# Attention inside a four-layer hybrid model on one core: a unit's transpositions stand one cycle later, and its probabilities lie in free rows of another pool

## The chip, the cores and the metric

The kernel runs on one core of a Trainium2 chip, in one launch. The metric is the device time in microseconds of one execution, and the number compared is the median over several runs.

The engines have these names in the profile: PE is TensorE's matmul, PEld its weight loads, DVE is VectorE, ACT is ScalarE, POOL is GpSimd, and SP issues most of the DMAs. Each engine works through its own instructions in the order in which they stand, and waits for the others by semaphores.

## What is computed

A token sequence of 16 meta tokens and 1024 tokens passes through four layers with residual additions: sliding-window attention, mLSTM, HGRN2, and sliding-window attention again. All arithmetic is float32; the kernel forms a float32 product as three products of split operands (high by high, high by low, low by high). Only the two attention layers matter here. Cut to the mixing itself:

```python
A_HEADS, A_KV, A_HD, BLOCK = 16, 4, 64, 128

def sliding_window_attention(q, k, v, sinks, valid):
    # qb: [bsz, nb, BLOCK, A_KV, g, A_HD]; kk, vv: the block before and the block itself
    s = jnp.einsum('bnqhgd,bnkhd->bnhgqk', qb, kk) * (A_HD ** -0.5)
    s = jnp.where(mask[None, :, None, None], s, -jnp.inf)       # causal band of 128 tokens
    sink = sinks.astype(jnp.float32).reshape(A_KV, g, 1)
    m = jnp.maximum(s.max(axis=-1), sink)
    e = jnp.exp(s - m[..., None])
    p = e / (e.sum(axis=-1) + jnp.exp(sink - m))[..., None]
    o = jnp.einsum('bnhgqk,bnkhd->bnqhgd', p, vv)
    return o.reshape(bsz, lp, A_W)
```

Around it stand an RMS norm, the projections to q, k, v and a gate z, norms and rotary positions on q and k, `o * silu(z)`, and the projection back to 1024 columns.

## The kernel before

**How the work is tiled.** Tokens stand in three chunks of 400, 384 and 256 columns, and in nine blocks for the attention: block 0 has the 16 meta tokens, blocks 1 to 8 have 128 tokens each. Heads are taken four at a time. A *unit* is one block of queries and one *pair*: two q tiles `t` of 128 features with two heads each (`hh` 0 and 1, indexed by feature half; `u` 0 and 1, indexed by tile). Four pairs by nine blocks are 36 units in the first attention layer; the last layer leaves block 0 out and has 32.

**What a unit does.** Three steps, which the code calls by letters:

- `S_step` (the scores): PE makes the scores of the four heads in two PSUM banks `pm` (L959). POOL copies the heads' sinks beside the place of the scores (L969). DVE adds the mask and scales into the SBUF tile `Sm`, with the row minimum of the negated scores (L972, one instruction and a small read-out for each head). ACT takes the exponential with the row sum (L977, once for each head). DVE inverts the four sums (L979), and POOL multiplies the rows by them (L982, once for each `hh`, two heads at a time). What is then in `Sm` are the probabilities.
- `T_step` (the transpositions): for each `hh`, PE transposes the probabilities through the identity (L998), up to four matmuls of 128 columns, into a PSUM bank `pt`; ACT rounds them to the high part `Ph` (L1000) and DVE subtracts for the low part `Pl` (L1001).
- `V_step` (the values): PE multiplies v by `Ph` and `Pl` into `po` (L1016). After the last block of a group, ACT and DVE move the sums into the output rows `R["o", t]` (L1024, L1025).

**What sets the order.** PE's order is written out by the program: `mixers()` makes a list of steps with costs, in which empty steps with a cost are pauses, and `weave` merges that list with the *fill*, the projections of the same layer (L271 for q, k, v and z, L569 for the projection back), in proportion to the costs. So the pauses only say how much fill stands between two steps. One cycle of the list before, for the unit `d` whose scores are made and the unit `e` ahead of it:

```python
seg += both(432, T_step, e)
if d:
    seg.append([1000, hi(lambda d=d: S_step(d)), None])
seg.append([V_WAIT, lambda: None, None])     # 1000
seg += both(480, V_step, e)
if d:
    seg.append([T_WAIT, lambda: None, None])  # 1500
```

The other engines' orders are made from the same program by a scheduler with priorities. It also hands out buffers. `Sm` comes from the layer's own pool with 2 buffers, one for each `hh`, so that the next unit's sinks and scores wait until the transpositions of the unit ahead have read them. `row()` is another pool: eight rows of 1040 float32 columns, tag "r", that hold k's high and low parts, the output rows of the pairs under way, working rows of k's projection in the first layer, and some weights.

Of the kernel before, what the change touches and what calls it, by code (L numbers as in the profile page):

```python
# [9 lines left out]
F32 = mybir.dt.float32  # L10
F32R = mybir.dt.float32r
AF = mybir.ActivationFunctionType
ALU = mybir.AluOpType
PSUM = bass.MemoryType.PSUM

P = 128
D = 1024
KT = D // P
NMETA = 16
# [10 lines left out]
def blk(b):  # L30
    return (0, NMETA) if b == 0 else (NMETA + P * (b - 1), P)
# [13 lines left out]
KT_LAG, ATT_LAG = 1400.0, 600.0  # L45
NORM_AT = (4000.0, 0.7), (5000.0, 0.5), (8000.0, 0.5)
Y_LAST, Y_EARLY, Y_AHEAD = 3, 8, 2500.0
V_WAIT, T_WAIT = 1000.0, 1500.0
D_V, V_AHEAD, K_AHEAD = 1500.0, 6500.0, 12000.0
FIRST = (1.1, 0.2, 0.85), (2.1, 1.35, 1.85)  # L50
D_K0, D_K1 = (4300.0, 6300.0, 8300.0), (4400.0, 5700.0, 6700.0)
# [70 lines left out]
def hybrid_kernel(ctx: ExitStack, tc: tile.TileContext, ins, out, layers=(0, 1, 2, 3)):  # L122
    nc = tc.nc
    v, s, g, pe, sp = nc.vector, nc.scalar, nc.gpsimd, nc.tensor, nc.sync
# [11 lines left out]
    def nm(x):  # L136
        ctr[0] += 1
        return f"{x}{ctr[0]}"

    def row():  # L140
        return rpool.tile([P, T], F32, tag="r", name=nm("r"), bufs=ROWS)
# [10 lines left out]
    def small(w):  # L152
        return tpool.tile([P, w], F32, tag=f"s{w}", name=nm("s"), bufs=12 if w < 8 else 4)

    def psum(tag, bufs):
        return ps.tile([P, 512], F32, tag="p", name=nm(tag), bufs=8)
# [59 lines left out]
    def new_mix():  # L216
        if layer_pool[0] is not None:
            layer_pool[0].close()
        layer_pool[0] = ExitStack()
        return layer_pool[0].enter_context(tc.tile_pool(name=nm("mix"), bufs=1))  # L220
# [59 lines left out]
    def hi(fn):  # L280
        def f():
            with tc.high_priority(offset=PRIO):
                fn()

        return f
# [442 lines left out]
    def layer_a(i, j, first, last, fin, scale=None):  # L728
        win, wout = ins["a_win"][j], ins["a_wout"][j]
        chunks = LAST_CHUNKS if last else CHUNKS  # L730
        R = {}

        def enter():
            R["mix"] = mix = new_mix()
            R["masks"] = masks = mix.tile([P, 384], F32, name=nm("masks"))
            sp.dma_start(masks, ins["a_masks"])
            R["cons"] = cons = mix.tile([P, 18], F32, name=nm("cons"))
            sp.dma_start(cons, ins["a_cols"][j])
            v.tensor_scalar(cons[:, 0:1], cons[:, 0:1], -0.125, None, op0=ALU.mult)
            v.tensor_scalar(cons[:, 2:18], cons[:, 2:18], -1.0, None, op0=ALU.mult)  # L740
# [45 lines left out]
        def idle(n, c0, cn):  # L786
            z = [R["mix"].tile([P, 2, 2, P], F32, tag=z, name=nm(z), bufs=2) for z in ("Ph", "Pl")]
            z = [y.rearrange("p a u q -> p (a u q)") for y in z]
            z.append(R["mix"].tile([P, 2, 257], F32, tag="Sm", name=nm("Sm"), bufs=2).rearrange("p u k -> p (u k)"))
            return [y[:, :cn] for y in z]  # L790

        def qk_proj(src, gcol, work, fsplit, ch, t=None, fetched=False):
# [142 lines left out]
        def mixers():  # L935


            def S_step(d):
                mix, cons = R["mix"], R["cons"]
                b, n, pair, ts = d[0]["b"], d[0]["n"], d[0]["pair"], d[0]["ts"]  # L940
                q0, nq = blk(b)
                kq = CHUNK_BLOCKS[n].index(b)
                qb = slice(q0 - chunks[n][0], q0 - chunks[n][0] + nq)
                if b == 0:
                    k0, kbs = 0, ((0, 0, 16),)
                elif b == 1:
                    k0, kbs = 0, ((0, 0, 16), (1, 16, 128))
                else:
                    k0, kbs = q0 - P, ((b - 1, 0, 128), (b, 128, 128))
                nk = sum(z[2] for z in kbs)  # L950
                kw, mo = (nk if b == 0 else 256), {0: 128, 1: 112}.get(b, 0)
                S = [psum("pm", 2).rearrange("p (u k) -> p u k", u=2) for _ in range(2)]
                k = R["k", pair // 2]
                for u, t in enumerate(ts):
                    q = R["q", t, n]
                    for i, (x, y) in enumerate(((0, 0), (0, 1), (1, 0))):
                        for hh in range(2):
                            hs = slice(64 * hh, 64 * hh + 64)
                            pe.matmul(S[hh][:nq, u, :kw], q[x][hs, qb], k[y][hs, k0 : k0 + kw],  # L959
                                      start=(i == 0), stop=(i == 2))  # L960
                st, den = small(8), small(8)
                for w in d:
                    hh = w["hh"]
                    w["kbs"] = kbs
                    w["Sm"] = Sm = mix.tile([P, 2, 257], F32, tag="Sm", name=nm("Sm"), bufs=2)
                    if b == 0:
                        g.memset(Sm[:, :, :NMETA], 0.0)
                    head = (2 * (ts[0] // 4) + hh) * 4 + ts[0] % 4
                    g.tensor_copy(Sm[:nq, :, nk : nk + 1], cons[:nq, 2 + head : 4 + head].rearrange("p (u c) -> p u c", c=1))  # L969
                    for u in range(2):  # L970
                        rq = R["rq", ts[u], n][:nq, 2 * kq + hh : 2 * kq + hh + 1]
                        v.tensor_tensor_reduce(Sm[:nq, u, :nk], S[hh][:nq, u, :nk], R["masks"][:nq, P + mo : P + mo + nk],  # L972
                                               rq, cons[:nq, 2 + head + u : 3 + head + u], ALU.add, ALU.min,
                                               st[:nq, 2 * hh + u : 2 * hh + u + 1])
                    for u in range(2):
                        z = slice(2 * hh + u, 2 * hh + u + 1)
                        s.activation(Sm[:nq, u, : nk + 1], Sm[:nq, u, : nk + 1], AF.Exp, scale=-1.0,  # L977
                                     bias=st[:nq, z], accum_out=den[:nq, z])
                v.reciprocal(den[:nq, :4], den[:nq, :4])  # L979
                for w in d:  # L980
                    hh, Sm = w["hh"], w["Sm"]
                    g.tensor_tensor(Sm[:nq, :, :nk], Sm[:nq, :, :nk],  # L982
                                    den[:nq, 2 * hh : 2 * hh + 2].rearrange("p (u c) -> p u c", c=1).to_broadcast([nq, 2, nk]),
                                    op=ALU.mult)

            def T_step(w):
                b, kbs, Sm = w["b"], w["kbs"], w["Sm"]
# [39 lines left out]
            units = []  # L1027
# [6 lines left out]
            def both(cost, fn, d):  # L1034
                return [[cost, hi(lambda w=w: fn(w)) if w else lambda: None, None] for w in d or (None, None)]

            for k in range(len(units) + 1):
                d = units[k] if k < len(units) else None
                e = units[k - 1] if k else None
                seg = segs[d[0]["pair"] if d else 4]  # L1040
                seg += both(432, T_step, e)
                if d:
                    seg.append([1000, hi(lambda d=d: S_step(d)), None])
                    if d[0]["b"] == CHUNK_BLOCKS[d[0]["n"]][-1]:
                        order["S", d[0]["pair"], d[0]["n"]] = seg[-1]
                seg.append([V_WAIT, lambda: None, None])
                seg += both(480, V_step, e)
                if d:
                    seg.append([T_WAIT, lambda: None, None])
            return segs  # L1050

        zc = {t: gate_proj(win[12 + t], lambda t=t: R["o", t], chunks, scale) for t in range(8)}
# [18 lines left out]
        head, ev = [], []  # L1071
        for n in range(3):
# [9 lines left out]
            head.append(grp)  # L1082
        hang = ev
        head[0].insert(0, [0.0, enter, None])
        sp1, out1 = outs(oc[1])
        sp3, out3 = outs(oc[3])
# [7 lines left out]
        ]  # L1094
        body = []
        segs = mixers()
        for p, ahead in enumerate((V_AHEAD, 0.0, K_AHEAD, 0.0)):
            segs[p].insert(0, [ahead, lambda: None, None])
# [5 lines left out]
        for i in range(3, 12):  # L1104
            for t in (2 * (i // 3), 2 * (i // 3) + 1):
                at = [id(z) for z in body]
                q, k = (at.index(id(z)) if id(z) in at else -1
                        for z in (order["q", t, i % 3], order["S", i // 3 - 1, i % 3]))
                if q < k:
                    z, d = body.pop(q), 0.0  # L1110
# [737 lines left out]
    for pos, i in enumerate(layers):  # L1848
# [10 lines left out]
        if i % 3 == 0:  # L1859
            head, body, oa, ob = layer_a(i, i // 3, tail is None, i == 3, fin, norm if tail is None else None)  # L1860
        elif i % 3 == 1:
            head, body, oa, ob = layer_b(i, i // 3, fin)
        else:
            head, body, oa, ob = layer_c(i, i // 3, fin)
        if tail is not None:
# [6 lines left out]
            h0, h1 = (sum(z[0] for z in head[k]) for k in range(2))  # L1872
            seq += flat(head)
            for n, start, end in ((2, t_b, t_b + h0 + h1), (1, t_a, t_b + h0), (0, 0.0, t_b)):
                d, share = NORM_AT[n]
                t0 = skip + start + d
                norm.place(seq, n, t0, t0 + 600.0, t0 + 600.0 + share * (skip + end - t0 - 600.0))
            head = [seq]
        else:
# [10 lines left out]
            head = [seq]  # L1890
# [16 lines left out]
    ahead, k = 0.0, 0  # L1907
# [120 lines left out]
```

## Time and profile before

| | |
|---|---|
| median of 3 runs | 2573.05 us (2572.45 to 2578.16) |
| the profiled execution: its own time | 2573.78 us |
| the profiled execution: its span | 2572.0 us |
| mean granted TensorE clock | 0.996 |
| first attention layer, units under way | from 59 us to about 425 us |
| last attention layer, units under way | from about 2168 us to 2505 us |

The span is what the profile covers, from the first instruction to the last; the execution's own time is 1.8 us longer. In the profile's rows, "x" gives a count. In a table of waits the columns are the total in us, how often, and the longest. In the table by stretches of time there are, after the bounds and the length, the busy us of each engine with the count of its instructions, then PEclk, the TensorE clock that was granted (1.00 is full), the share of the DMA engines and GB/s. A busy PE is not PE at its peak, and "idle before" is counted from the modelled end of the matmul ahead.

### The profile page before, as it was taken

What the parts mean: (1) busy time and instruction counts of PE and PEld (TensorE: products, weight loads), DVE (VectorE), ACT (ScalarE), POOL (GpSimd) and SP (SyncE); (2) the same over time, 40 slices, a digit from 0 to 9 for tenths busy, and PEclk for the clock granted to TensorE, in tenths of its full rate; (3) what the DMA queues carried; (4) which work ended last, traced back from release to release, by engine and by line L of the source; (5) the groups of instructions that cost most, each with busy time, mean ns of one, the idle gap of its engine ahead of it and who ended that gap; (6) DMA issues with size and microseconds to landing.
All of it is one profiled execution on the core that took longest, in us unless ns stands there. A gap on an engine that the chain in (4) does not pass through costs nothing.

```text
span 2572.0 us, 55550 instructions
## 1 busy us (share of the span) xinstructions
PE 2517.3 (98%) x20424; PEld 2438.9 (95%) x20424; DVE 2122.4 (83%) x5804; ACT 1733.9 (67%) x4679; POOL 252.1 (10%) x569
## 2 busy tenths in 40 slices
PE   9899999999999999999999999999999999999999
PEld 8799998999999999999999999999999999899989
DVE  7786887988979889789887798888878988787876
ACT  7665767576877778778772248887676856756672
POOL 0321222000000000000000001100000100321220
PEclk9999999999999999999999999999999999999999
DMA  5113222212212222221242211110111113112212
GB/s 164 51 55 89 60 64 65 87 53 50 71 45 73 68 55 62 59 73 52 84 126 91 66 50 35 35 40 30 43 35 43 39 47 100 50 49 76 60 34 82
DMA packets 113714, 161.58 MB, mean 63 GB/s; under 512 B 16521, under 2 KB 65810, under 8 KB 113442
## 3 DMA queue, kind: packets, MB, share of 16 engines
q1 hardware_dynamic: 113154, 157.51, 20.5%
q8 instruction: 161, 2.64, 0.4%
q14 instruction: 111, 0.91, 0.1%
q10 hardware_dynamic: 288, 0.52, 0.1%
HBM read 132.48 MB, written 14.92 MB: 57 GB/s over the span
## 4 chain that ended last, share of the span: by engine, by line
PE 58%; DVE 20%; ACT 13%; DMA 4%; issue 3%; POOL 1%; SPq 0%; DVEq 0%; POOLq 0%; ACTq 0%
PE pj L271 17%; PE pj L569 15%; PE pj L387 9%; PE pj L530 4%; PE pj L472 2%; DMA wr<-in_b_win 2%; ACT Sm L977 2%; PE pt L998 2%; DVE wl L231 2%; ACT wh L230 1%; POOL Sm L982 1%; ACT t L706 1%; ACT t L705 1%; PE po L1016 1%; PE pm L959 1%
## 5 line engine op out<-in xcount | busy, mean ns | idle before, releaser
L271 PE MATMUL pj<-uh,wh 128*128 128x384 f32 (+2 forms) x1680 | 572.9, 341 | 1.8 <-ACT uh L646 1.0
L271 PE MATMUL pj<-ul,wh 128*128 128x384 f32 (+2 forms) x1680 | 540.3, 322 | 1.5 <-DVE ul L647 1.0
L271 PE MATMUL pj<-uh,wl 128*128 128x384 f32 (+2 forms) x1680 | 539.9, 321 | 0.0
L271 PEld LDWEIGHTS pj<-uh,wh 128*128 128x128 f32 x1680 | 317.6, 189 | 15.1 <-issue 2.2
L271 PEld LDWEIGHTS pj<-ul,wh 128*128 128x128 f32 x1680 | 318.2, 189 | 5.6 <-DVE ul L647 1.6
L271 PEld LDWEIGHTS pj<-uh,wl 128*128 128x128 f32 x1680 | 317.4, 189 | 0.3 <-DVE wl L231 0.3
L231 DVE TENSOR_TENSOR wl<-wr,wh 128x512 fp32r<-128x512 f32 (+1 forms) x336 | 239.1, 721 | 72.5 <-ACT wh L230 69.0
L230 ACT CAST wh<-wr 128x512 fp32r<-128x512 f32 (+1 forms) x336 | 202.6, 614 | 90.4 <-DMA wr<-in_b_win 24.3
L572 DVE TENSOR_TENSOR x<-x,pj 128x384 f32<-128x384 f32 (+2 forms) x480 | 234.2, 510 | 35.0 <-PE pj L569 33.6
L569 PE MATMUL pj<-yh,wh 128*128 128x384 f32 (+2 forms) x768 | 253.8, 330 | 4.3 <-DVE x L572 4.0
L569 PE MATMUL pj<-yl,wh 128*128 128x384 f32 (+2 forms) x768 | 246.0, 320 | 0.3 <-DVE yl L231 0.3
L387 PE MATMUL pj<-uh,wh 128*128 128x384 f32 (+1 forms) x756 | 244.5, 323 | 1.3 <-ACT t L585 1.0
L569 PE MATMUL pj<-yh,wl 128*128 128x384 f32 (+2 forms) x768 | 245.3, 319 | 0.0
L387 PE MATMUL pj<-uh,wl 128*128 128x384 f32 (+1 forms) x756 | 238.7, 316 | 0.2 <-DVE wl L231 0.2
L387 PE MATMUL pj<-ul,wh 128*128 128x384 f32 (+1 forms) x756 | 238.4, 315 | 0.0
L982 POOL TENSOR_TENSOR Sm<-Sm,s 128x512 f32<-128x512 f32 (+2 forms) x136 | 143.4, 1075 | 433.3 <-DVE s L979 417.5
L977 ACT ACTIVATE Sm<-Sm,s 128x257 f32<-128x257 f32 (+2 forms) x272 | 129.8, 479 | 73.9 <-DVE s L972 72.7
L230 ACT CAST yh<-r 128x384 fp32r<-128x384 f32 (+2 forms) x120 | 57.0, 479 | 163.5 <-PE pj L569 146.5
L569 PEld LDWEIGHTS pj<-yh,wh 128*128 128x128 f32 x768 | 144.4, 188 | 7.9 <-DVE x L572 4.6
L708 ACT ACTIVATE t<-t 128x384 f32<-128x384 f32 (+3 forms) x240 | 117.7, 491 | 50.6 <-DVE t L707 48.8
L530 PE MATMUL pj<-wh,uh 128*128 128x256 f32 (+1 forms) x504 | 145.9, 290 | 0.0
L569 PEld LDWEIGHTS pj<-yl,wh 128*128 128x128 f32 x768 | 144.6, 188 | 1.0 <-DVE yl L231 0.7
(378 smaller groups left out, 6971.8 us busy)
## 6 DMA issues: line engine op xcount, KB each, us to landing
wr<-in_b_win SPq DMA_DIRECT2D x124, 256.0 KB, 2.8
wr<-in_a_win SPq DMA_DIRECT2D x78, 256.0 KB, 2.9
wr<-in_c_win SPq DMA_DIRECT2D x64, 256.0 KB, 2.6
wr<-in_a_wout SPq DMA_DIRECT2D x32, 256.0 KB, 3.0
rw<-rowsd SPq DMA_DIRECT2D x64, 128.0 KB, 3.7
wr<-in_b_wout SPq DMA_DIRECT2D x32, 256.0 KB, 2.8
parked<-r SPq DMA_DIRECT2D x12, 520.0 KB, 2.6
r<-parked SPq DMA_DIRECT2D x12, 520.0 KB, 3.5
```

The costliest lines, as they stand in the source:

```text
L230: s.copy(h, src)
L231: v.tensor_tensor(l, src, h.bitcast(F32), op=ALU.subtract)
L271: pe.matmul(acc[:, :cn], a[:, k, :], b[:, k, c0 : c0 + cn], start=(k == 0 and i == 0), stop=(k == KT - 1 and i == 2))
L387: pe.matmul(acc[key][:, :n], p, q, start=(first and z == 0 and i == 0), stop=(last and z == 1 and i == 2))
L472: pe.matmul(acc[:, :cn], a[:, kk, :], m[:, k, :cn], start=(k == 0 and j == 0), stop=(k == KT - 1 and j == 2))
L530: pe.matmul(acc[:cn, :nc], a[:, k, c0 : c0 + cn], m[:, kk, :], start=(k == 0 and j == 0), stop=(k == KT - 1 and j == 2))
L569: pe.matmul(acc[:, :cn], a[:, k, mc], b, start=(k == 0 and i == 0), stop=(k == 1 and i == 2))
L572: v.tensor_tensor(xt(m, c0, cn), xt(m, c0, cn), acc[:, :cn], op=ALU.add)
L708: s.activation(a[:, :cn], a[:, :cn], AF.Exp)
L977: s.activation(Sm[:nq, u, : nk + 1], Sm[:nq, u, : nk + 1], AF.Exp, scale=-1.0, bias=st[:nq, z], accum_out=den[:nq, z])
L982: g.tensor_tensor(Sm[:nq, :, :nk], Sm[:nq, :, :nk], den[:nq, 2 * hh : 2 * hh + 2].rearrange("p (u c) -> p u c", c=1).to_broadcast([nq, 2, ...
L998: pe.transpose(pt[:kn, ki, u, :], Sm[:, u, ko : ko + kn], ident)
```

## The change

Three things are done.

1. The cycle's order becomes scores of unit `k`, values of unit `k-2`, transpositions of unit `k-1`, with pauses of 500, 500 and 800 between them. Before, it was transpositions of `k-1`, scores of `k`, values of `k-1`. A unit's transpositions and values thus come one cycle later against its scores, and there is one cycle more at the end of the layer.
2. The probabilities of the four heads lie in one row of the pool of eight (`row()`), as four pieces of 257 columns. The tile `Sm` of the layer's pool is gone.
3. POOL copies the four sinks in one instruction and multiplies the four heads in one instruction, where there were two of each. `cons` gets two more columns so that the four sinks can be named in one slice, and a scratch tile of the first layer that shared `Sm`'s tag has a tag of its own.

```diff
-V_WAIT, T_WAIT = 1000.0, 1500.0
+UNIT = 500.0, 500.0, 800.0
...
-            R["cons"] = cons = mix.tile([P, 18], F32, name=nm("cons"))
+            R["cons"] = mix.tile([P, 20], F32, name=nm("cons"))
+            cons = R["cons"][:, :18]
...
-            z.append(R["mix"].tile([P, 2, 257], F32, tag="Sm", name=nm("Sm"), bufs=2).rearrange("p u k -> p (u k)"))
+            z.append(R["mix"].tile([P, 400], F32, tag="idle", name=nm("idle"), bufs=2))
...
                 st, den = small(8), small(8)
+                Sm = row()[:, : 4 * 257].rearrange("p (a k) -> p a k", a=4)
+                if b == 0:
+                    g.memset(Sm[:, :, :NMETA], 0.0)
+                h0 = 2 + 8 * (ts[0] // 4) + ts[0] % 4
+                sinks = cons[:nq, h0 : h0 + 8].rearrange("p (h u) -> p h u", h=2)[:, :, :2]
+                g.tensor_copy(Sm[:nq, :, nk : nk + 1].rearrange("p (h u) c -> p h u c", h=2)[:, :, :, 0], sinks)
                 for w in d:
                     hh = w["hh"]
                     w["kbs"] = kbs
-                    w["Sm"] = Sm = mix.tile([P, 2, 257], F32, tag="Sm", name=nm("Sm"), bufs=2)
-                    if b == 0:
-                        g.memset(Sm[:, :, :NMETA], 0.0)
-                    head = (2 * (ts[0] // 4) + hh) * 4 + ts[0] % 4
-                    g.tensor_copy(Sm[:nq, :, nk : nk + 1], cons[:nq, 2 + head : 4 + head].rearrange("p (u c) -> p u c", c=1))
+                    w["Sm"] = Sm[:, 2 * hh : 2 * hh + 2]
...
                 v.reciprocal(den[:nq, :4], den[:nq, :4])
-                for w in d:
-                    hh, Sm = w["hh"], w["Sm"]
-                    g.tensor_tensor(Sm[:nq, :, :nk], Sm[:nq, :, :nk],
-                                    den[:nq, 2 * hh : 2 * hh + 2].rearrange("p (u c) -> p u c", c=1).to_broadcast([nq, 2, nk]),
-                                    op=ALU.mult)
+                g.tensor_tensor(Sm[:nq, :, :nk], Sm[:nq, :, :nk],
+                                den[:nq, :4].rearrange("p (a c) -> p a c", c=1).to_broadcast([nq, 4, nk]), op=ALU.mult)
...
-            for k in range(len(units) + 1):
-                d = units[k] if k < len(units) else None
-                e = units[k - 1] if k else None
+            def pause(t):
+                return [t, lambda: None, None]
+
+            for k in range(len(units) + 2):
+                d, e, f = (units[k - z] if 0 <= k - z < len(units) else None for z in range(3))
                 seg = segs[d[0]["pair"] if d else 4]
-                seg += both(432, T_step, e)
                 if d:
                     seg.append([1000, hi(lambda d=d: S_step(d)), None])
...
-                seg.append([V_WAIT, lambda: None, None])
-                seg += both(480, V_step, e)
-                if d:
-                    seg.append([T_WAIT, lambda: None, None])
+                seg.append(pause(UNIT[0]))
+                seg += both(480, V_step, f)
+                seg.append(pause(UNIT[1]))
+                if k <= len(units):
+                    seg += both(432, T_step, e) + [pause(UNIT[2])]
```

What moves on PE, at one unit of the first pair in the first attention layer (block 3). Names: `pm` are scores, `pt` transpositions, `po` values, `pj` projections, and the number is the buffer's. Before, from the end of the unit's scores to its transpositions (`Sm_1133`, `Sm_1139`) there stand three stretches of six projection matmuls and the eight matmuls of the values of the unit ahead; the next unit's scores follow at once:

```order
L959 MATMUL pm_1118<-r_512,qs_408 128x256
...
L1016 MATMUL po_1068<-Ph_1085,v_858 128x2x128
...
L1016 MATMUL po_1073<-Pl_1110,v_861 128x2x128
...
L271 MATMUL pj_1179<-uh,wl_1052 128x400
L998 MATMUL pt_1192<-ident,Sm_1133 128x128 x4
L998 MATMUL pt_1201<-ident,Sm_1139 128x128 x4
L959 MATMUL pm_1210<-r_512,qs_546 128x256
```

The same unit in the change has its probabilities in `r_1095`. Between its scores and its transpositions there now stand five stretches of six projection matmuls, two steps of values, the transpositions of the unit ahead (`r_974`) and the next unit's scores (`pm_1163`):

```order
L960 MATMUL pm_1080<-r_512,qs_408 128x256
...
L1015 MATMUL po_1122<-Ph_1047,v_850 128x2x128
...
L997 MATMUL pt_1139<-ident,r_974 128x128 x4
L997 MATMUL pt_1148<-ident,r_974 128x128 x4
...
L960 MATMUL pm_1163<-r_512,qs_546 128x256
...
L1015 MATMUL po_1122<-Ph_1140,v_854 128x2x128
...
L997 MATMUL pt_1239<-ident,r_1095 128x128 x4
L997 MATMUL pt_1248<-ident,r_1095 128x128 x4
```

So the transpositions were put behind one whole further cycle. On POOL, whose work on two neighbouring units stands like this before, copies of the sinks for one unit always follow the products of the unit ahead:

```order
L969 COPY Sm_1226<-cons_216 128x2
L969 COPY Sm_1232<-cons_216 128x2
L982 TENSOR_TENSOR Sm_1226<-Sm_1226,s_1225 128x2x256
L982 TENSOR_TENSOR Sm_1232<-Sm_1232,s_1225 128x2x256
L969 COPY Sm_1327<-cons_216 128x2
L969 COPY Sm_1333<-cons_216 128x2
```

In the change one copy and one product are left for each unit, and where rows are free the copies stand two units ahead of the products:

```order
L968 COPY r_1283<-cons_216 128x4
L918 MEMSET v_3295 128x258
L982 TENSOR_TENSOR r_1095<-r_1095,s_1094 128x4x256
L968 COPY r_1370<-cons_216 128x4
L982 TENSOR_TENSOR r_1179<-r_1179,s_1178 128x4x256
L968 COPY r_1484<-cons_216 128x4
```

The work is the same, in half as many instructions, and the copy no longer stands between one unit's product and the next unit's scores.

More of the change, by code (lines that the diff above doesn't have):

```diff
@@ L964, in S_step @@
                     w["kbs"] = kbs
-                    w["Sm"] = Sm = mix.tile([P, 2, 257], F32, tag="Sm", name=nm("Sm"), bufs=2)
-                    if b == 0:
-                        g.memset(Sm[:, :, :NMETA], 0.0)
-                    head = (2 * (ts[0] // 4) + hh) * 4 + ts[0] % 4
-                    g.tensor_copy(Sm[:nq, :, nk : nk + 1], cons[:nq, 2 + head : 4 + head].rearrange("p (u c) -> p u c", c=1))
+                    w["Sm"] = Sm[:, 2 * hh : 2 * hh + 2]
                     for u in range(2):
                         rq = R["rq", ts[u], n][:nq, 2 * kq + hh : 2 * kq + hh + 1]
[L972 to L979, printed above, removed]
-                for w in d:
-                    hh, Sm = w["hh"], w["Sm"]
-                    g.tensor_tensor(Sm[:nq, :, :nk], Sm[:nq, :, :nk],
-                                    den[:nq, 2 * hh : 2 * hh + 2].rearrange("p (u c) -> p u c", c=1).to_broadcast([nq, 2, nk]),
-                                    op=ALU.mult)
+                        z = 2 * hh + u
+                        v.tensor_tensor_reduce(Sm[:nq, z, :nk], S[hh][:nq, u, :nk], R["masks"][:nq, P + mo : P + mo + nk],
+                                               rq, sinks[:, hh, u : u + 1], ALU.add, ALU.min, st[:nq, z : z + 1])
+                    for z in (2 * hh, 2 * hh + 1):
+                        s.activation(Sm[:nq, z, : nk + 1], Sm[:nq, z, : nk + 1], AF.Exp, scale=-1.0,
+                                     bias=st[:nq, z : z + 1], accum_out=den[:nq, z : z + 1])
+                v.reciprocal(den[:nq, :4], den[:nq, :4])
+                g.tensor_tensor(Sm[:nq, :, :nk], Sm[:nq, :, :nk],
+                                den[:nq, :4].rearrange("p (a c) -> p a c", c=1).to_broadcast([nq, 4, nk]), op=ALU.mult)
             def T_step(w):
```

## The prediction

> **What bounds the kernel now.** I read the page first, then the waits of PE, then stretches of time, then the order of time around single waits. The page's first line says that PE is the engine to look at:
>
> ```profile
> PE 2517.3 (98%) x20424; PEld 2438.9 (95%) x20424; DVE 2122.4 (83%) x5804; ACT 1733.9 (67%) x4679; POOL 252.1 (10%) x569
> ```
>
> PE stands idle for 2572.0 − 2517.3 = 54.7 us of the span. The list of waits says for whom:
>
> ```profile
> PE pt L998 <- POOL Sm L982: 27.4, 37, 2.4
> PE pj L569 <- DVE x L572: 4.0, 3, 1.4
> ...
> PEld pt L998 <- POOL Sm L982: 39.8, 46, 2.7
> ```
>
> Half of PE's idle time is one wait: the transpositions wait for POOL's product with the inverted sums. The next one is a seventh of it. POOL is busy for 10% of the span, so it is late and not full: it is the last link of a chain. The table by stretches shows where this is:
>
> ```profile
> core 0: us, PE busy (x) PEld busy (x) DVE busy (x) ACT busy (x) POOL busy (x), PEclk, DMA share, GB/s
> 60.00:140.00 80.00, 70.33 (x493) 63.33 (x492) 58.31 (x172) 50.71 (x165) 24.87 (x40) 0.91 0.19 53
> 140.00:300.00 160.00, 159.07 (x1123) 150.06 (x1124) 123.12 (x319) 101.27 (x288) 32.63 (x62) 1.00 0.24 70
> 300.00:345.00 45.00, 42.94 (x312) 40.52 (x312) 37.44 (x96) 30.09 (x92) 12.86 (x16) 1.00 0.26 76
> 345.00:425.00 80.00, 71.33 (x528) 65.15 (x527) 69.87 (x187) 52.41 (x154) 25.62 (x44) 1.00 0.14 43
> 2170.00:2230.00 60.00, 55.51 (x423) 50.70 (x422) 46.77 (x131) 41.55 (x131) 20.84 (x31) 1.00 0.20 58
> 2230.00:2430.00 200.00, 199.36 (x1433) 191.83 (x1432) 155.35 (x385) 130.34 (x368) 44.50 (x65) 1.00 0.22 64
> 2430.00:2500.00 70.00, 65.30 (x481) 59.45 (x481) 57.56 (x154) 46.92 (x131) 19.46 (x33) 1.00 0.08 23
> ```
>
> PE idles where units are dense, in the first and the last pair of both attention layers, and hardly at all between them, where more fill lies between two units. DVE's column matters later: 69.87 of 80 us in the fourth row is close to full.
>
> **Part 1, the transpositions one cycle later.** One wait in order of time (PE, with POOL's product):
>
> ```profile
> 77.27 0.34 PE L271 MATMUL pj<-ul,wh 128*128 128x400 f32 x1
> 77.45 0.34 PE L271 MATMUL pj<-uh,wl 128*128 128x400 f32 x1
> 79.36 0.66 PE L998 MATMUL pt<-ident,Sm 128*128 128x128 f32 x4 [1.56 <-POOL Sm L982]
> ...
> 81.16 0.60 PE L998 MATMUL pt<-ident,Sm 128*128 128x128 f32 x4
> 81.69 0.98 PE L959 MATMUL pm<-r,qs 64*128 64x256 f32 x12
> 82.60 0.45 PE L271 MATMUL pj<-uh,wh 128*128 128x400 f32 x1
> ...
> 83.80 0.28 PE L1016 MATMUL po<-Ph,v 128*128 128x256 f32 x1
> ...
> 84.73 0.34 PE L271 MATMUL pj<-uh,wh 128*128 128x400 f32 x1
> ...
> 86.75 0.34 PE L271 MATMUL pj<-uh,wl 128*128 128x400 f32 x1
> 89.49 0.90 PE L998 MATMUL pt<-ident,Sm 128*128 128x128 f32 x3 [2.40 <-POOL Sm L982]
> ...
> 88.40 2.03 POOL L982 TENSOR_TENSOR Sm<-Sm,s 128x512 f32<-128x512 f32 x2 [6.32 <-DVE s L979]
> ```
>
> Projection matmuls start 0.18 us apart (77.27, 77.45), so PE could have begun at 77.63, and began at 79.36: 1.73 us lost, where the list says 1.56. At 89.49 it is 2.56 (from 86.75 + 0.18) against 2.40. Each wait costs some 0.17 more than listed, because the idle time is counted from the modelled end. 37 waits: 27.4 + 37 × 0.17 = 33.7 us. (The weight loads' 39.8 also counts nine short waits that PE's own column does not show, so it is an upper bound.)
>
> Does the slack suffice? From the end of the scores (82.60) the second product is ready at 88.40 + 2.03 = 90.43, a chain of 7.8 us. Before, PE has 18 projection matmuls (18 × 0.18 = 3.3) and eight for values (84.73 − 83.80 = 0.9) to put in between: 4.2 us. In the change it is 30 × 0.18 = 5.4, twice 0.9, the next scores (82.60 − 81.69 = 0.9) and eight transpositions (twice 81.69 − 81.16, so 1.1): 9.2 us. The wait should go where the chain stays below 9.2; the margin is 1.4 us, and some waits will stay. I give back 3 us for them: one of the longest, or ten of 0.3. The values follow their transpositions as far behind as before. ACT's cast and DVE's subtraction lie beside the scores and the fill between, and the values waited for them only once:
>
> ```profile
> PE po L1016 <- DVE Pl L1001: 0.5, 1, 0.5
> ```
>
> I price that at nothing; with that cover gone in all 34 units of the dense pairs it would be 34 × 0.5 = 17 us. The extra cycle at the end of a layer lies beside the gate projections of the last pair, which are all still to be done: nothing too.
>
> **The clock.** The two longest waits have a tail:
>
> ```profile
> 84.00:88.00 4.00, 3.09 (x20) 2.75 (x18) 2.81 (x10) 3.88 (x13) 0.00 (x0) 1.00 0.11 30
> 88.00:92.00 4.00, 2.51 (x12) 1.91 (x14) 0.86 (x2) 1.51 (x5) 2.40 (x4) 0.67 0.08 21
> 92.00:96.00 4.00, 4.00 (x34) 3.87 (x33) 3.47 (x13) 2.40 (x10) 0.00 (x0) 0.90 0.00 0
> ...
> 120.00:124.00 4.00, 1.65 (x12) 1.06 (x10) 3.00 (x6) 2.72 (x9) 1.91 (x2) 0.94 0.00 0
> 124.00:128.00 4.00, 3.53 (x21) 3.29 (x22) 3.75 (x6) 2.38 (x5) 1.35 (x3) 0.50 0.53 152
> 128.00:132.00 4.00, 4.00 (x23) 3.78 (x20) 3.25 (x13) 2.18 (x9) 0.37 (x1) 0.50 0.26 79
> 132.00:136.00 4.00, 4.00 (x26) 4.00 (x26) 0.60 (x1) 1.25 (x5) 2.36 (x4) 0.78 0.00 0
> ```
>
> The granted clock falls right behind each of them and comes back later. Lost: 4 × (0.33 + 0.10) = 1.7 us and 4 × (0.06 + 0.50 + 0.50 + 0.22) = 5.1 us, 6.8 together. If the waits go, I expect the clock to stay.
>
> **Part 2, rows in place of `Sm`.** No instruction is added. In a layer's first pair three or four rows go round, so a unit's sinks are copied while an older unit is still to be transposed; in the late pairs mostly two alternate, and the copy waits for transpositions that stand ahead of its unit's scores on PE. Two weight tiles and the output rows come from the same pool; their loads are issued ahead of need, the weights' by up to 12 us of PE work, which is longer than the 7.8 us chain. Price: nothing; a load that comes too late for want of a row would cost up to one such chain, 7.8 us a layer.
>
> **Part 3, one product in place of two.** POOL's columns:
>
> ```profile
> L982 POOL TENSOR_TENSOR Sm<-Sm,s 128x512 f32<-128x512 f32 x112 | 130.2, 1183 | 296.7 <-DVE s L979 296.7
> L969 POOL COPY Sm<-cons 128x2 f32<-128x2 f32 x128 | 35.0, 274 | 144.0 <-PE pt L998 129.5 <-DVE cons L740 14.2
> ```
>
> One product should take about twice 1.0 us (2.03 for the pair at 88.40; the mean of 1.18 has time in which POOL is held). Of the copies half go, 64 × 0.27 us. POOL is off the bound, so neither counts; what counts is DVE beside it:
>
> ```profile
> 111.67 2.71 POOL L982 TENSOR_TENSOR Sm<-Sm,s 128x512 f32<-128x512 f32 x2 [4.01 <-DVE s L979]
> 112.09 1.40 DVE L862 TENSOR_TENSOR t<-t,cs 128x384 f32<-128x384 f32 x1
> 113.52 1.27 DVE L863 TENSOR_TENSOR t<-t,t 128x384 f32<-128x384 f32 x1
> ...
> L862 DVE TENSOR_TENSOR t<-t,cs x51: 395/551/1395, 31.1 to 2429.8; 128x384 f32<-128x384 f32 x25, 128x256 f32<-128x256 f32 x17, 128x400 f32<-128x400 f32 x9
> ```
>
> Two DVE operations of 0.55 us took 1.40 and 1.27 while POOL worked: 1.6 us lost to two products. A single product of 2.0 us can hold one DVE operation for at most 2.0, so up to 0.4 us worse where two were held already, 1.0 where one was; or better, if DVE is then on scores from PSUM. The ends are −1.6 and +1.0 a unit. It matters only where DVE is near full, the 18 dense units of the first layer; I take 18 × 0.17 = 3 us, nearest to the row where two are held.
>
> **DVE's floor.** The best that DVE shows while PE hardly waits, and PE's waits for POOL from 345 to 425:
>
> ```profile
> 160.00:180.00 20.00, 19.34 (x136) 18.17 (x135) 19.11 (x48) 14.39 (x40) 6.03 (x8) 1.00 0.14 44
> 180.00:200.00 20.00, 19.73 (x149) 18.82 (x149) 18.44 (x48) 9.16 (x29) 4.89 (x6) 1.00 0.10 32
> ...
> PE pt L998 <- POOL Sm L982: 7.7, 9, 1.7
> ```
>
> DVE is busy for 37.55 of 40 us, 0.94. Without waits the stretch 345 to 425 would last 80 − 9.2 = 70.8 us (nine waits, 7.7 + 9 × 0.17), but DVE's 69.87 us need 69.87 / 0.94 = 74.3: 3.5 us come back. From 60 to 140, 58.31 / 0.94 = 62.0 against 80 − 9.67 − 6.8 = 63.5: nothing. Other stretches have more room.
>
> **Sum.** −33.7 − 6.8 + 3 (waits that stay) + 3 (product) + 3.5 (DVE) = −31.0. From the profiled execution's own 2573.8 us that is 2542.8; the median of the runs is 0.7 below that execution, so 2542.
>
> **Rivals.**
>
> *DVE becomes the bound.* In 345 to 425 it idled 10.1 of 80 us. If 0.87 is all that it can do in dense stretches, they need 58.31 / 0.87 = 67.0 (3.5 back from 60 to 140), 80.3 (all 9.2 back) and 57.56 / 0.87 = 66.2 from 2430 to 2500 against 70 − 4.7 = 65.3 (0.9 back): 13.6 in place of 3.5, so 2552. For it: the handing back and forth with ACT. Against it: the 0.94 above.
>
> *The clock falls anyway.* No wait exceeds 2.4 us, and the 1.56 us at 79.36 left the clock at 1.00 (row 84 to 88); if the two falls have another cause, 6.8 us stay: 2549. For it: only two of 37 waits are followed by a fall. Against it: they are the two longest. The Trainium skill (TensorE: Matmul & The Clock Gate, "What's actually happening") has the clock halved after an idle window of some 3.4 us. By that rule alone waits of 2.4 us would not lower it, and the sum would be this rival's; the trace shows the fall behind them.
>
> *All of it comes.* No stay, no loss: 2573.1 − 40.5 = 2533.
>
> *The chain grows with the slack.* If DVE, pressed by a faster PE, lengthens the chain from 7.8 to over 9.2 + 1.7 us, the transpositions wait as before and the change does not do what it says: about 2573.
>
> *Slower: the long product holds DVE.* One mechanism, at L982: each of 64 full units holds a two-operand DVE operation for a whole product of 2.0 us in place of half of it, 1.0 more, and PE waits for that operation: 64 − 40.5 = +24, so 2597. It decides from 40.5 / 64 = 0.63 us a unit. Against it: in the long middle stretches DVE is busy for 77%, and PE's fill covers 1 us. The Trainium skill (SBUF — State Buffer, "SBUF: two separate sides") says that the two engines lock each other out of a shared pair of ports for a whole instruction; the two held operations above agree.
>
> **How the numbers follow.** Chances: the forecast 0.53, DVE 0.17, clock 0.10, all of it 0.07, grown chain 0.07, long product 0.06. The first four end faster: 0.87. About 0.2% (5 us) is what a measurement of this kernel can tell from no change; the grown chain gives 0.06 within it and 0.01 beyond, and the long product is the rest of slower, 0.07. For 8 in 10 the range takes the full gain with 2 us beyond, 2531, and on the other side the DVE and clock rivals together (2552 + 6.8 = 2559) and 3 us of the product's upper end, 2562; outside lie about 0.18.
>
> **What the profile after would show.** Part 1 is right if the transpositions' wait for POOL falls from 27.4 to under 5 us; the clock if no stretch from 60 to 140 falls below 1.0; part 3 if products read about 2.1 us, and DVE's two-operand forms keep their means; DVE's floor if PE's waits for DVE grow mostly in 345 to 425. I am wrong if scores or values take over as PE's longest wait, or if projections wait for PSUM buffers that DVE frees late.

## The result, and the profile after

| | before | after |
|---|---|---|
| median, 4 runs each | 2572.86 us (2572.45 to 2578.16) | 2545.73 us (2543.44 to 2547.95) |
| after / before | | 0.9890, 95% interval 0.9873 to 0.9907 |
| profiled execution, its own time | 2573.78 us | 2545.87 us |
| span, mean granted clock | 2572.0 us, 0.996 | 2544.1 us, 0.998 |

The change makes the kernel 1.1% faster, 27 us where 31 were forecast. First line of the page after:

```profile
PE 2509.5 (99%) x20424; PEld 2438.6 (96%) x20424; DVE 2131.1 (84%) x5804; ACT 1730.7 (68%) x4679; POOL 208.1 (8%) x429
```

PE's idle time fell from 54.7 to 34.6 us. DVE is busy for 8.7 us more, with as many instructions: some of them got slower. PE's longest waits after (total, count, longest):

```profile
PE pj L569 <- DVE x L572: 5.7, 5, 1.5
PE po L1758 <- DVE S L1742: 3.1, 5, 1.0
PE pj L271 <- DVE Pl L1000: 1.9, 1, 1.9
PE po L1015 <- DVE Pl L1000: 1.8, 3, 0.7
PE pj L569 <- DVE yl L231: 1.4, 1, 1.4
PE pm L960 <- DVE Pl L1000: 1.4, 3, 0.8
```

The transpositions' wait for POOL (27.4 us, 37 times) is gone without a remainder; no row of PE's whole list names POOL, and the six longest all name DVE. POOL's groups after (busy, mean ns, idle before and its releasers):

```profile
L982 POOL TENSOR_TENSOR r<-r,s 128x1024 f32<-128x1024 f32 x56 | 109.2, 1950 | 367.1 <-DVE s L981 356.2 <-DVE rq L840 10.9
L968 POOL COPY r<-cons 128x4 f32<-128x4 f32 x64 | 18.9, 301 | 150.0 <-DVE yl L231 64.8 <-DMA t<-t 42.6 <-PE pt L997 35.7
```

The copies, which waited 129.5 us for transpositions, wait 35.7. The same stretches of time as before (the work in them has moved up by what was gained ahead of them):

```profile
60.00:140.00 80.00, 78.12 (x583) 73.62 (x582) 67.23 (x196) 58.33 (x192) 20.81 (x28) 0.98 0.26 73
140.00:300.00 160.00, 156.59 (x1108) 146.66 (x1107) 123.90 (x319) 100.28 (x283) 24.16 (x30) 1.00 0.23 67
300.00:345.00 45.00, 42.39 (x301) 39.84 (x301) 38.37 (x98) 26.79 (x84) 9.98 (x12) 0.96 0.18 51
345.00:425.00 80.00, 79.32 (x586) 75.71 (x585) 69.60 (x180) 58.98 (x160) 18.07 (x23) 1.00 0.23 70
2230.00:2430.00 200.00, 197.92 (x1430) 189.33 (x1430) 163.66 (x396) 126.13 (x358) 34.38 (x33) 1.00 0.20 60
2430.00:2500.00 70.00, 68.68 (x491) 66.47 (x490) 58.31 (x133) 53.37 (x133) 11.84 (x10) 1.00 0.14 46
```

PE gained 7.8 us of 80 in the first row and 8.0 in the fourth, where the waits were. It lost in the middle, where it had hardly waited: 2.5 of 160 and 1.4 of 200. The clock still falls in the first attention layer, in two places:

```profile
96.00:100.00 4.00, 2.12 (x11) 2.04 (x12) 3.97 (x10) 1.00 (x3) 0.72 (x2) 0.86 0.39 106
100.00:104.00 4.00, 4.00 (x23) 4.00 (x22) 3.07 (x11) 2.81 (x12) 1.06 (x1) 0.71 0.15 41
...
336.00:340.00 4.00, 2.83 (x20) 2.62 (x21) 3.94 (x10) 1.17 (x3) 0.00 (x0) 0.73 0.00 0
340.00:344.00 4.00, 4.00 (x26) 3.94 (x25) 3.92 (x17) 1.75 (x10) 0.48 (x2) 0.85 0.00 0
```

That is 4 × (0.14 + 0.29) = 1.7 us and 4 × (0.27 + 0.15) = 1.7 us, 3.4 in place of 6.8. Elsewhere a fall of 1.7 us at 4 to 12 us is gone, and one of 1.7 us at 632 to 640 is new, so over the whole span the difference is the same 3.4. The order of time on POOL, DVE and PE at the first fall shows what is late now:

```profile
94.35 1.89 POOL L982 TENSOR_TENSOR r<-r,s 128x1024 f32<-128x1024 f32 x1 [4.63 <-DVE s L981]
94.94 1.73 DVE L862 TENSOR_TENSOR t<-t,cs 128x400 f32<-128x400 f32 x1 [0.68 <-DMA t<-t]
95.49 1.05 PE L835 MATMUL pa<-masks,t 128*128 128x2 f32 x8
96.60 0.56 DVE L863 TENSOR_TENSOR t<-t,cs 128x400 f32<-128x400 f32 x1
97.19 0.57 DVE L864 TENSOR_TENSOR t<-t,t 128x400 f32<-128x400 f32 x1
97.68 1.28 DVE L1000 TENSOR_TENSOR Pl<-pt,Ph 128x512 fp32r<-128x512 f32 x2
98.42 0.44 PE L271 MATMUL pj<-uh,wh 128*128 128x384 f32 x1 [1.88 <-DVE Pl L1000]
```

POOL's product runs from 94.35 to 96.24. L862 starts inside it and takes 1.73 us, where its neighbours L863 and L864 take 0.56 and 0.57; it ends 0.4 us after the product. Below I call this a *hold*: a DVE instruction stretched by a POOL instruction that runs beside it. Behind it in DVE's queue stands the subtraction to `Pl`, which frees a PSUM bank, and the next projection waits for that bank. A product that no longer makes the transpositions wait makes PE wait through DVE. The second fall has a hold ahead of it too: POOL's product runs from 333.57 to 335.46, L862 on 128x256 starts at 334.44 and takes 1.30 us (0.42 on average where the product is on ACT), and at 336.34 the scores wait for the DVE instruction behind it.

### The profile page after: what moved, and what is told of

It reads as the page before. It is cut to its first block, busy times and chain, and to the rows that moved or that the text cites. A ratio compares the mean times of both kernels' runs of the same rounds, so it can differ in the third digit from the quotient of the medians.

```text
span 2544.1 us, 55227 instructions
## 1 busy us (share of the span) xinstructions
PE 2509.5 (99%) x20424; PEld 2438.6 (96%) x20424; DVE 2131.1 (84%) x5804; ACT 1730.7 (68%) x4679; POOL 208.1 (8%) x429
## 4 chain that ended last, share of the span: by engine, by line
PE 64%; DVE 18%; ACT 11%; DMA 4%; issue 2%; SPq 1%; DVEq 0%; ACTq 0%
PE pj L271 16%; PE pj L569 16%; PE pj L387 14%; PE pj L530 5%; PE pj L472 3%; DVE wl L231 2%; PE po L1274 1%; ACT r L979 1%; PE pm L960 1%; PE po L1015 1%; PE pt L997 1%; ACT wh L230 1%; ACT t L706 1%; ACT t L705 1%; DVE t L707 1%
## 5 line engine op out<-in xcount | busy, mean ns | idle before, releaser
L979 ACT ACTIVATE r<-r,s 128x257 f32<-128x257 f32 (+2 forms) x272 | 129.7, 479 | 70.3 <-DVE s L976 69.9
L982 POOL TENSOR_TENSOR r<-r,s 128x1024 f32<-128x1024 f32 (+2 forms) x68 | 120.6, 1773 | 461.8 <-DVE s L981 450.7
```

Of the source, the lines that this page charges most:

```text
L979: s.activation(Sm[:nq, z, : nk + 1], Sm[:nq, z, : nk + 1], AF.Exp, scale=-1.0, bias=st[:nq, z : z + 1], accum_out=den[:nq, z : z + 1])
L982: g.tensor_tensor(Sm[:nq, :, :nk], Sm[:nq, :, :nk], den[:nq, :4].rearrange("p (a c) -> p a c", c=1).to_broadcast([nq, 4, nk]), op=ALU.mult)
```

## The experiments

Each ran in five rounds beside the kernel before. In short (the ratio is to the kernel before, in the same series):

| run | median, us | ratio, 95% interval |
|---|---|---|
| changed kernel, again | 2547.52 | 0.9888 (0.9870 to 0.9907) |
| order alone | 2563.18 | 0.9962 (0.9949 to 0.9974) |
| rows alone, old order | 2597.26 | 1.0089 (1.0075 to 1.0103) |
| changed, less slack | 2555.17 | 0.9931 (0.9919 to 0.9943) |
| changed, two products | 2537.47 | 0.9858 (0.9845 to 0.9872) |
| changed, four products | 2532.09 | 0.9830 (0.9814 to 0.9846) |
| changed, products on ACT | 2546.39 | 0.9888 (0.9869 to 0.9906) |
| changed, four scalar products | 2528.03 | 0.9813 (0.9798 to 0.9829) |
| before, scalar products | 2619.98 | 1.0183 (1.0169 to 1.0197) |
| before, two waits filled | 2571.46 | 0.9985 (0.9976 to 0.9993) |

### The order without the rows

The diff is the change's lines in `mixers()` and `UNIT`, and nothing else; `Sm` keeps its two buffers.

> Only the order of the change (scores of k, values of k-2, transpositions of k-1, with its pauses), on the old buffers: two tiles Sm, two copies and two products a unit. A unit's scores can then be taken from PSUM only after the transpositions of the unit ahead, which now stand behind this unit's scores. Theory (the room in the rows is needed): the slack between the release of Sm and the unit's own transpositions is one cycle, 18 x 0.18 + 8 x 0.11 + 0.9 = 5.1 us in dense stretches against a chain of 7.8 us, so most of the 37 waits stay, each 0.9 us shorter than before (4.2 us of slack before): 27.4 us of waits become about 10 to 15, and 2555 to 2562 us. Rival 1 (the order alone does it): 2542 to 2549, waits for POOL's product under 3 us. Rival 2 (scores now wait in PSUM and hold its banks, so that projections wait as well): 2573 or more.

2563.18 us. Three of PE's waits, and then DVE's group of score instructions (busy, mean ns, idle before and its releasers):

```profile
PE pm L959 <- DVE s L972: 5.8, 9, 1.1
PE pj L569 <- DVE s L972: 3.2, 3, 2.0
...
PE pt L998 <- POOL Sm L982: 0.3, 1, 0.3
```

```profile
L972 DVE CUSTOM_DVE_ANT_0 Sm<-pm,masks,cons 128x256 f32<-128x256 f32 (+2 forms) x272 | 127.0, 513 | 16.2 <-PE pt L998 12.4 <-POOL Sm L982 2.2 <-POOL Sm L967 0.2
```

The time is near the theory's, its mechanism is not: the transpositions hardly wait for POOL. DVE waits 12.4 us for transpositions that free `Sm`, and the scores wait for the banks that DVE frees (5.8 us), projections for the same DVE instructions (3.2 us). That is the second rival's mechanism at a smaller price. The order takes the old wait away; without room it turns part of it into a new one.

### The rows without the order

Parts 2 and 3 of the change, with the loop of before.

> The change without its order: probabilities in a row, one copy and one product a unit, in the old order (transpositions of k-1, scores of k, values of k-1). Theory (the gain comes from the slack that the order makes, and the rows by themselves bring none): PE still waits about 37 times, and the first transposition now waits for one product of 1.9 us where it waited for the first of two (1.0 us), while the second no longer waits: 0 to 0.9 us more a wait, so 0 to +33 us; I expect about +8, 2573 to 2590. Rival (the copy of the sinks, which waited 129 us for transpositions, was what made the chain long, and free rows take that out): waits fall by half, 2550 to 2560.

2597.26 us: above the 2573 to 2590 that I expected, within the 33 us that the theory allowed. PE's wait:

```profile
PE pt L997 <- POOL r L982: 44.8, 34, 3.3
```

34 waits of 1.3 us on average in place of 37 of 0.74: in the old order the first transposition waits for the whole long product. Rows and the single product were not tried apart in the old order, so this +22 us is theirs together. From order alone to order, rows and two products it is 25.7 us the other way: with the order the rows are worth much. What rows with two products bring in the old order was not run.

### Less slack

```diff
-                seg.append(pause(UNIT[0]))
-                seg += both(480, V_step, f)
-                seg.append(pause(UNIT[1]))
                 if k <= len(units):
-                    seg += both(432, T_step, e) + [pause(UNIT[2])]
+                    seg += both(432, T_step, e) + [pause(UNIT[0])]
+                seg += both(480, V_step, f) + [pause(UNIT[1] + UNIT[2])]
```

> The changed kernel with the transpositions of k-1 ahead of the values of k-2 in the cycle (scores of k, transpositions of k-1, pause, values of k-2, longer pause); buffers and product as changed. At the unit of block 3 there then stand 24 projection matmuls in place of 30 and one step of values in place of two between its scores and its transpositions: 24 x 0.18 + 0.9 + 0.9 + 1.1 = 7.2 us of slack where the prediction counted 9.2. Theory (the longest chain is 7.8 us, typical ones 5 to 6): the transpositions wait for POOL again, but only in the longest units, 2 to 8 us in all, and the time is 2548 to 2556. Rival 1 (chains in the faster kernel are as long as the slack given): 15 us of waits and more, over 2560. Rival 2 (the margin was larger than needed): no such waits, and within 3 us of the changed kernel, 2543 to 2549.

2555.17 us, as the theory had it, and the wait is back in a few units:

```profile
PE pt L997 <- POOL r L982: 6.2, 7, 3.1
```

So the slack of the changed kernel, 9.2 us as counted at block 3, suffices for every unit, and about 7.2 does not.

### Two products, and four

```diff
-                g.tensor_tensor(Sm[:nq, :, :nk], Sm[:nq, :, :nk],
-                                den[:nq, :4].rearrange("p (a c) -> p a c", c=1).to_broadcast([nq, 4, nk]), op=ALU.mult)
+                for hh in range(2):
+                    z = slice(2 * hh, 2 * hh + 2)
+                    g.tensor_tensor(Sm[:nq, z, :nk], Sm[:nq, z, :nk],
+                                    den[:nq, z].rearrange("p (a c) -> p a c", c=1).to_broadcast([nq, 2, nk]), op=ALU.mult)
```

With four, the loop runs over the heads.

> The changed kernel with two products of 128x512 a unit in place of one of 128x1024; all else as changed. Theory of the prediction (a long product can hold one DVE instruction longer, but only where DVE is near full): 0 to 3 us faster than the changed kernel, 2543 to 2546. Rival 1 (two products are dearer in all, 2 x 1.18 against 1.95 us, and each holds a DVE instruction of its own): 2 to 8 us slower than the changed kernel, 2548 to 2554. Rival 2 (what POOL does is hidden): within 2 us of it.

> The changed kernel with four products of 128x256 a unit, one for each head, in place of one of 128x1024. Theory (a product holds a two-operand DVE instruction until it ends, so a shorter product holds less: DVE was busy for 2131 us with one product and 2116 with two): DVE's busy time 2108 to 2116 us and 2533 to 2541 us in all. Rival 1 (each product holds an instruction of its own, so that the number counts and two is the best): DVE 2118 to 2130, 2540 to 2550. Rival 2 (the chain of the four, about 4 x 0.65 = 2.6 us, comes too late): waits of the transpositions for POOL come back, over 5 us in all.

2537.47 us with two products, 8 less than with one, where the theory gave up to 3. Its size was too small and the first rival's sign was wrong. Four gave 2532.09, a microsecond better than that theory's 2533 to 2541. The page's first line with two, then with four:

```profile
PE 2507.6 (99%) x20424; PEld 2437.4 (96%) x20424; DVE 2116.3 (83%) x5804; ACT 1730.9 (68%) x4679; POOL 227.9 (9%) x497
```

```profile
PE 2502.4 (99%) x20424; PEld 2433.6 (96%) x20424; DVE 2109.4 (83%) x5804; ACT 1731.1 (68%) x4679; POOL 257.2 (10%) x633
```

POOL works longer the more pieces there are (208, 228, 257 us) and DVE shorter (2131, 2116, 2109), with the same instructions. That fits a hold that ends with the one POOL instruction beside it. The single product, part 3 of the change, cost 8 us against two, not 3.

### The product on ACT, and as a scalar form on POOL

```diff
+                for z in range(4):
+                    s.activation(Sm[:nq, z, :nk], Sm[:nq, z, :nk], AF.Copy, scale=den[:nq, z : z + 1])
...
+                for z in range(4):
+                    g.tensor_scalar(Sm[:nq, z, :nk], Sm[:nq, z, :nk], den[:nq, z : z + 1], None, op0=ALU.mult)
```

Each in place of the product of the changed kernel.

> The changed kernel with the product on ACT: four activations of 128x256 with the inverted sum as scale, 4 x 0.45 = 1.8 us, as long as POOL's one. POOL then holds nothing but the copies of the sinks. Theory (the held DVE instructions are what the single product costs): DVE's busy time falls by 15 to 25 us, to 2106 to 2116, and where ACT has room the time falls by 8 to 15, 2531 to 2538. Rival (ACT takes the place of DVE as the engine waited for: 64 x 1.8 = 115 us more on ACT, 1731 to 1846 us, and in the dense stretches 0.74 + 0.1 of them): PE waits for ACT by 10 us and more, 2550 to 2570.

> The changed kernel with POOL's product in another form: four instructions of 128x256 that take the inverted sum as a scalar for each partition, in place of one with two tensors of 128x1024. Theory (a hold lasts as long as one POOL instruction, whatever its form): as four products, DVE 2108 to 2116 us, 2533 to 2541 us. Rival 1 (only POOL's form with two tensors holds DVE): DVE's two-operand forms at their free durations, 0.55 for 128x400, DVE at 2100 to 2108, 2528 to 2535. Rival 2 (this form is slow on POOL, over 1 us each): the chain grows to 10 us and more, and the transpositions wait for POOL again by 10 us or more, 2555 to 2575.

The page's first line with the product on ACT, then with the scalar form:

```profile
PE 2512.6 (99%) x20424; PEld 2440.9 (96%) x20424; DVE 2093.7 (82%) x5804; ACT 1825.9 (72%) x4951; POOL 90.5 (4%) x361
```

```profile
PE 2499.4 (99%) x20424; PEld 2431.5 (96%) x20424; DVE 2097.3 (83%) x5804; ACT 1732.0 (69%) x4679; POOL 339.8 (13%) x633
```

On ACT, DVE's time falls by 37 us, more than the theory gave, and the whole time stays, between the theory's and the rival's: PE is idle for 36.9 us, its longest single wait is now 3.0 us for ACT, and what it gained from DVE it lost elsewhere (which waits took how much was not taken apart). The scalar form is the fastest, 2528.03 us. POOL works most in it, and still DVE is within 4 us of what it takes with no product on POOL. POOL and DVE in order of time, scalar form, at the place where the changed kernel's first fall was:

```profile
92.75 4.40 POOL L983 TENSOR_SCALAR r<-r,s 128x256 f32<-128x256 f32 x4 [2.85 <-DVE s L981]
92.68 0.58 DVE L862 TENSOR_TENSOR t<-t,cs 128x400 f32<-128x400 f32 x1
93.17 0.57 DVE L863 TENSOR_TENSOR t<-t,cs 128x400 f32<-128x400 f32 x1
93.77 0.65 DVE L864 TENSOR_TENSOR t<-t,t 128x400 f32<-128x400 f32 x1
```

Three two-operand instructions run beside POOL's products at about their free duration; POOL's four take 4.40 us here against 3.63 in many other units. There is no wait of PE at this place, and the mean granted clock is 1.000. The theory (any POOL instruction holds) falls; the first rival was right, with DVE 2.7 us below its range: the form with two tensors holds DVE, the scalar form hardly does.

### The scalar form in the kernel before

> The kernel before with POOL's product in the scalar form alone: four instructions of 128x256 in place of two of 128x512, old order and old tiles. It takes about 1.0 us for each head, so 2.0 us until the first transposition may start in place of 1.2, and 4.0 in place of 2.4 until the second. Theory (in the old order POOL's product lies on the path of PE, and only the later transpositions take it off): DVE's busy time falls by 20 to 25 us (2122 to about 2100), yet the 37 waits grow by 0.4 to 1.2 us each, and the time is 2585 to 2615. Rival (held DVE instructions were a good part of the chain): the chain grows by less than the holds gave back, 2565 to 2575.

2619.98 us, beyond the theory's end. PE's wait:

```profile
PE pt L998 <- POOL Sm L984: 46.9, 84, 2.2
```

19.5 us more of waits, 47 × 0.17 = 8 us for their tails, and a mean granted clock of 0.989 in place of 0.996 (0.007 × 2618, some 18 us). DVE was busy for 21 us less, and the time still rose. The slower product is best only where the slack covers it.

### Two waits filled

```diff
-                pt = psum("pt", 1).rearrange("p (k u q) -> p k u q", k=2, u=2)
+                pt = psum("pt", 1)
+                if first and w["pair"] == 0 and w["hh"] == 0 and b in (3, 7):
+                    kk = R["k", 0][0]
+                    for _ in range(14):
+                        pe.matmul(pt[:, :384], kk[:, 0:128], kk[:, 0:384], start=True, stop=True)
+                pt = pt.rearrange("p (k u q) -> p k u q", k=2, u=2)
```

> The kernel before, and 14 matmuls of 384 columns, whose results nobody uses, in front of the transpositions of blocks 3 and 7 of the first pair in the first layer: 14 x 0.17 = 2.4 us of PE work in each of the two long waits of 2.4 us. The waits for POOL stay where they are, only PE is not idle in them. Theory (the idle time lowers the granted clock): no stretch from 84 to 136 us falls below 1.0 and the kernel is up to 6.8 us faster, 2566 to 2571. Rival (the falls have another cause): the same falls at the same places, 2573 within 2 us.

2571.46 us, 0.07 to 0.24% faster. The stretches where the clock fell before, and what follows:

```profile
88.00:92.00 4.00, 3.67 (x29) 2.85 (x28) 1.25 (x2) 1.40 (x3) 2.34 (x4) 1.00 0.05 13
...
124.00:128.00 4.00, 4.00 (x39) 3.76 (x38) 4.00 (x11) 1.91 (x5) 0.00 (x0) 1.00 0.50 163
128.00:132.00 4.00, 1.98 (x15) 1.76 (x14) 3.30 (x10) 3.67 (x15) 2.04 (x2) 0.96 0.01 5
132.00:136.00 4.00, 4.00 (x29) 3.83 (x29) 2.56 (x7) 1.94 (x6) 0.99 (x5) 0.61 0.28 78
```

Both falls are gone with the idle time, as the theory had it. The time alone does not decide, since 2571.46 is also within 2 us of the rival's 2573; the kernel before took 2575.47 beside it. It stays just above what the theory gave because the clock fell at four other places in this execution, by 1.7 us each. The first is behind the next unit's wait (2.02 us, ending at 131.05): 4 × (0.04 + 0.39) = 1.7 us. The others, at 408 to 416, 648 to 656 and 2196 to 2204, stand behind waits that the kernel before has too, of the same length within 0.01 us, and there the clock stayed at 1.00. So one execution does not show which wait will have a fall. Over the traces the two go together: the scalar form in the old order has PE idle for 73.8 us and loses 27 us to falls, four products and four scalar products in the new order have 26.9 and 25.7 us of idle time and no fall.

## Why the prediction came out as it did

The forecast was 2542, the median 2545.73, inside the range. By its steps:

- *The transpositions' waits, −33.7.* Right, all of it. The 3 us for waits that stay were not needed: none stayed. The run with less slack shows that the arithmetic of slack against chain was good to a microsecond or two. Counted from start to start of PE's matmuls (beyond the usual spacing of the same form, where that is over 0.25 us more), these waits took about 35 us before, so the tails were priced rightly as well.
- *The clock, −6.8.* Mis-sized by half: 3.4 us stay. The step that failed is "if the waits go, I expect the clock to stay". Other idle time of PE does the same: the wait of 1.88 us for DVE at 98.42, and at 336 to 338 several short ones. Both stand behind a hold, so this term is hardly apart from the next one: with four products and with the scalar form no stretch of 4 us in the profiled execution falls below 1.00. By size this is nearly the whole miss of 3.7 us. It also varies: the four executions had mean granted clocks of 0.998, 0.998, 0.997 and 1.000, and the one at 1.000 took 2543.44 us.
- *The single product, +3.* Right in mechanism and sign, too small: 8 us against two products, 17.7 against the scalar form, a part of each being the clock of the last point. I had put it only on the first layer's dense units. It is paid elsewhere too. DVE's subtraction `yl<-r,yh` on 128x384, the operand of the projections back, took 556 ns on average before, and 671, 616 and 569 with one, two and four products in the changed kernel, 556 with the scalar form and 555 with the product on ACT. With four products the stretch from 2230 to 2430, in the last layer, has 0.2 us of idle time left, where the changed kernel has 2.1:

```profile
2230.00:2430.00 200.00, 199.82 (x1448) 192.13 (x1449) 158.70 (x404) 126.82 (x360) 48.51 (x85) 1.00 0.21 61
```

- *DVE's floor, +3.5 in 345 to 425.* Wrong place. That stretch has PE busy for 79.32 of 80 us, and from 160 to 180 DVE goes up to 0.96:

```profile
160.00:180.00 20.00, 18.80 (x130) 17.35 (x130) 19.28 (x50) 9.73 (x29) 4.32 (x7) 1.00 0.04 14
```

"Other stretches have more room" was the mistake: DVE was as full in this one, and PE waited 1.2 us there. The row was already in the prediction: 19.11 of 20 us before.
- *The balance.* I gave back 3 + 3 + 3.5 = 9.5 us. By the same count from start to start, in both attention layers, waits other than the transpositions' went from about 8 to about 18 us, some 10 more. So the total was right with wrong shares, which is partly luck: −33.7 + 10 − 3.4 = −27.1 against 27.9 in the span.
- *The rows, 0.* As a price right: no wait of PE is for POOL's copy into a row or for a load. ACT does wait longer for the attention weights to arrive, 19.2 us in place of 8.3, for a reason that stays open. As a description too small: without them the order brings 10 us, with them (and two products) 37.
- *Rivals.* "DVE becomes the bound" named the engine that PE waits for now, "the clock falls anyway" happened by half in size, but behind new idle time and not behind another cause. "The long product holds DVE" is shown as a mechanism; at (2545.73 − 2528.03) / 64 = 0.28 us a unit it stays under the 0.63 from which it would have decided.
- *The signs.* Against the forecast: the clock fell within 60 to 140, DVE's two-operand forms did not all keep their means, PE's waits for DVE did not grow mostly in 345 to 425, and projections do wait for PSUM banks that DVE frees late (1.9 us at 98.42). The first sign, the transpositions' wait, came out as said; products read 1.95 us for 2.1.

## What to carry to other kernels

When a wait for a producer is long and the producer is idle, count what stands between the two on the waiting engine; one more cycle of distance needs a buffer for the cycle. Here the distance alone brought 10 us, buffers with the long product and no distance cost 22, and distance, buffers and two products brought 37. Then look at which engine the moved work runs beside: with the slack in hand the cheapest form of the product was the one that takes POOL longest (1.01 us for 256 columns against 0.70) and leaves DVE alone. The version to use is the changed kernel with four scalar products a unit, 2528.03 us, 0.9813 of the kernel before.

## What the runs showed of the hardware

- The length of one wait does not tell whether the granted clock falls. Between the attention layers the same two waits, 1.10 us and then 0.45 or 0.46 us, left it at 1.00 before and were followed by 0.85 and 0.73 after. PE in order of time and the stretches, before:

```profile
651.62 0.44 PE L1409 MATMUL pa<-yh,onesr 128*128 128x384 f32 x1 [1.10 <-ACT yh L230]
...
652.00:656.00 4.00, 3.54 (x21) 3.47 (x20) 3.93 (x10) 4.00 (x12) 0.00 (x0) 1.00 0.00 0
```

After:

```profile
633.19 0.44 PE L1410 MATMUL pa<-yh,onesr 128*128 128x384 f32 x1 [1.10 <-ACT yh L230]
...
632.00:636.00 4.00, 2.45 (x10) 2.11 (x10) 4.00 (x10) 4.00 (x12) 0.00 (x0) 0.85 0.00 0
636.00:640.00 4.00, 4.00 (x19) 4.00 (x18) 3.71 (x10) 4.00 (x12) 0.00 (x0) 0.73 0.00 0
```

With rows alone a wait of 2.58 us left it at 1.00 and one of 1.24 us was followed by 0.84 and 0.73:

```profile
81.59 0.66 PE L997 MATMUL pt<-ident,r 128*128 128x128 f32 x4 [2.58 <-POOL r L982]
...
109.44 0.66 PE L997 MATMUL pt<-ident,r 128*128 128x128 f32 x4 [1.24 <-POOL r L982]
```

```profile
84.00:88.00 4.00, 4.00 (x33) 3.86 (x33) 2.97 (x11) 2.70 (x9) 0.19 (x1) 1.00 0.04 12
...
108.00:112.00 4.00, 2.76 (x20) 2.23 (x20) 3.39 (x6) 2.20 (x6) 1.39 (x1) 0.84 0.50 134
112.00:116.00 4.00, 4.00 (x25) 3.78 (x26) 3.19 (x11) 3.04 (x11) 0.27 (x2) 0.73 0.06 13
```

Eight matmuls of two columns stand next to this wait (at 109.94) and next to the one in the changed kernel (at 95.49). They may count as idle, which was not tested; the two waits between the attention layers have none beside them. Each fall in the traces of this case lost about 1.7 us, or two or three times that (rows of 4 us, 1 − PEclk added up; a fall in the last 4 us, which the span cuts off, is left out). The Trainium skill (TensorE: Matmul & The Clock Gate, "What's actually happening") gives an idle window of some 3.4 us; falls here follow waits of 1.24, 1.88, 2.02 and 2.4 us, so as a length of one wait the traces disagree with it.
- POOL's product with two tensors holds a DVE instruction with two SBUF operands (L862: 1.73 us for 0.57); the scalar form, which also reads SBUF, hardly does. The Trainium skill (SBUF — State Buffer, "SBUF: two separate sides") has a DVE instruction with two SBUF inputs and any GpSimd instruction that reads SBUF lock each other out of shared ports; the first agrees with it, the scalar form here does not.
